# A decoder layer on one Trainium2 core: four-chunk groups with a PSUM bank a chunk, and the squares of x inside the opening group

## The chip, the cores and the metric

The kernel runs on one core of one Trainium2 chip. The metric is the time of one execution on the device, in microseconds (us); less is better. The engines are TensorE (PE in the profile; PEld is its weight load), VectorE (DVE), ScalarE (ACT), GpSimd (POOL) and SyncE (SP), whose queue issues most transfers.

## The reference

One layer of a decoder with 256 tokens of 1024 features, float32 throughout. Each of four sub-layers has an RMS norm before and after it, and is added to the residual stream:

```python
h = rmsnorm(x, ffn1_pre_g)                      # x * rsqrt(mean(x*x) + eps) * g
f = (silu(h @ w_gate) * (h @ w_up)) @ w_down    # D_FF = 2816
x = x + 0.5 * rmsnorm(f, ffn1_post_g)

h = rmsnorm(x, mix_pre_g)
proj = h @ w_in                                 # q, k, v (8 heads of 64) and pooling input
y = concatenate([moba_attention(q, k, v), multiscale_pool(p_in)]) @ w_out
x = x + rmsnorm(y, mix_post_g)

h = rmsnorm(x, xa_pre_g)                        # 4 heads of 256 over 256 memory tokens
x = x + rmsnorm(memory_cross_attention(h, rmsnorm(mem, mem_g)), xa_post_g)

# a second half-FFN like the first
```

## The kernel before, in words

Activations are held with features on partitions: a tensor of 1024 x 256 is eight chunks (ND = 8) of 128 features by 256 tokens (S). Every float32 operand of a product is split into a high and a low half, both in a reduced format (`fp32r`); a chunk of activations lies as 512 columns, high half in the first 256, low half in the other 256. A product of weight tile and chunk is then low weight x high activation, high weight x high activation and high weight x low activation.

**Weights** come as one stream of 128 x 128 tiles in the order in which they are used, in units of eight tiles (`UNIT`). The class `Weights` loads them (`_load`, on SP's queue), and `_make` (L76, L77) makes the high half by a cast on ScalarE and the low half by a subtraction on VectorE, some four units (`LEAD`) ahead of use. The first four units are loaded and split in parts by `open_in_parts` (L109, L112), together with the chunks of x (L188, L191).

**How products are formed.** `wide_chunk` makes one chunk of 128 output features in one PSUM bank: for two k at a time, two products of 256 columns by the low weights into the bank's second half (L210), then two of 512 columns by the high weights into the whole bank (L212). The second half is then added to the first, with a copy on ScalarE and an add on VectorE (L219, L220). `group` makes four chunks at a time, so that one k of the activations serves four tiles: two banks hold the four chunks, a half bank each, and a step of one k is twelve products of 256 columns (L266, L271, L273). There are three such groups, at the start of a stage, where the chunks of activations come one by one: the first two gate/up pairs of the first FFN (with the high weights first, since these are ready first), q of `w_in`, and four chunks of `xa_wq`. `row_step` forms products with the activations as weights and rows of 512 outputs, over four banks (L337 to L339).

**Norms.** The pre-norm's factor of a token isn't put into the activations; the products are scaled by it afterwards (`rBx`, made by `x_spread`). For the first FFN it comes from `x_squares` (three Squares on ScalarE, L579, and three adds on VectorE, L584) and `x_sums` (four products with a column of ones on TensorE, L590, and a root). `x_squares` is run in the code between the gate and the up half of f = 2, `x_sums` between those of f = 3, and `opened`, with `x_spread`, between those of f = 4.

**Order.** TensorE goes through its products in the order of the code everywhere. Between `seam(True)` and `seam(False)` all engines do; the opening, with its group, and the ends of rows (`row_end`, with the group that follows) lie there. Elsewhere a planner orders the other engines, by its own estimate of times. PSUM has eight banks: six in the pool of `accum`, two in that of `small`.

**Ends of rows.** `row_end` forms the post-norm of a stage, adds it to the residual, and transposes the result into the next stage's chunks: the first 128 tokens through small banks, the second 128 by `turned(i)`, four chunks at a time, between the halves of a filler pair of the memory tokens' keys.

`start` begins with seven plain products of zeros (`warm`, L542), each two passes in the trace, before the first weights are there.

Of the kernel before, what the change touches and what calls it, by code (L numbers as in the profile page):

```python
# [8 lines left out]
F32 = mybir.dt.float32  # L9
# [6 lines left out]
P = 128  # L16
D = 1024
S = 256
# [125 lines left out]
def build(nc, io, tiles_only=False):  # L144
# [3 lines left out]
    def small(name="sm"):  # L148
        return st["psm"].tile([P, 512], F32, name=name, tag="sm")

    def accum():
        return st["pacc"].tile([P, 512], F32, name="acc")

    def tmp(shape, name, **kw):
        return st["tmp"].tile(shape, F32, name=name, **kw)
# [28 lines left out]
    def halves(ps):  # L184
        return [ps[:, :S], ps[:, S:]]
# [21 lines left out]
    def wide(ps, ws, Xs, first, last):  # L207

        for i, (hi, lo) in enumerate(ws):
            nc.tensor.matmul(ps[:, S:], lo, Xs[i][:, :S], start=first and i == 0, stop=False, skip_group_check=True)  # L210
        for i, (hi, lo) in enumerate(ws):
            nc.tensor.matmul(ps, hi, Xs[i], start=False, stop=last and i == 1, skip_group_check=True)  # L212

    def wide_chunk(X, ps, o):

        for k in range(0, ND, 2):
            wide(ps, [st["w"].get() for _ in range(2)], [st[X][:, k + i, :] for i in range(2)], k == 0, k == ND - 2)
        c = tmp([P, S], "cmb")
        nc.scalar.copy(c, ps[:, S:])  # L219
        nc.vector.tensor_tensor(o, ps[:, :S], c, op=ALU.add)  # L220
# [37 lines left out]
    def group(name, X, cols, done, before=None, hi_first=False):  # L258

        def run():  # L260
            ps = [accum() for _ in range(2)]
            o = [h for p in ps for h in halves(p)]

            def by_lo(ws, k, first):
                for i, (hi, lo) in enumerate(ws):
                    nc.tensor.matmul(o[i], lo, st[X][:, k, :S], start=first and i % 2 == 0,  # L266
                                     stop=k == ND - 1 and hi_first, skip_group_check=True)

            def by_hi(ws, k, first):
                for i, (hi, lo) in enumerate(ws):  # L270
                    nc.tensor.matmul(o[i], hi, st[X][:, k, :S], start=first and i % 2 == 0,  # L271
                                     stop=False, skip_group_check=True)
                    nc.tensor.matmul(o[i], hi, st[X][:, k, S:], start=False,  # L273
                                     stop=k == ND - 1 and not hi_first, skip_group_check=True)
            steps = (by_hi, by_lo) if hi_first else (by_lo, by_hi)
            for k in range(ND):
                if before:
                    before(k)
                ws = [st["w"].get() for _ in cols]
                for i, by in enumerate(steps):  # L280
                    by(ws, k, k == i == 0)
            done(ps)
        names = [name] * len(cols) if isinstance(name, str) else name
        pr.add(run, [(n, k * P, c) for k in range(ND) for n, c in zip(names, cols)])
# [126 lines left out]
    def row_end(parts, ks, weights, factor, nxt, pre, fillers):  # L411
# [55 lines left out]
        def turned(i):  # L467
            def run():
                cs = range(4 * i, 4 * i + 4)
                x_turn(1, cs, accum)  # L470
                for c in cs:
                    x_hi(1, c)
                for c in cs:
                    x_lo(1, c)
            return run
# [54 lines left out]
    def start():  # L530
        X = st["xs_ffn1"] = xsplit()
        st["xf"] = keep([P, ND, S], "y")
        first = st["x0"] = st["ffn"].tile([P, 2 * S], F32, name="gu", bufs=6)
        n = S + len(GAINS) * ND
        nc.sync.dma_start(first[:, :n], io["first"])
        nc.gpsimd.memset(st["eps"], EPS)
        nc.gpsimd.memset(st["one"], 1.0)
        warm = tmp([P, S], "cmb")
        nc.vector.memset(warm, 0.0)
        ps = small("warm")  # L540
        for _ in range(7):
            nc.tensor.matmul(ps[:, :P], warm[:, :P], warm[:, :P], start=True, stop=True)  # L542

        def load(c):
            if c == 1:
                nc.scalar.preload_act_table(AF.Sqrt)
                nc.scalar.dma_start(st["xf"][:, 1:3, :], io["x"][:, 1:3, :])
            s = {2: slice(3, 5), 4: slice(5, 8)}.get(c)
            if s:
                nc.sync.dma_start(st["xf"][:, s, :], io["x"][:, s, :])  # L550

        def split(c):
            if c == 0:
                x, g = first[:, :S], first[:, S:S + 1]
                return (lambda: nc.vector.tensor_scalar(X[:, 0, :S], x, g, None, op0=ALU.mult),
                        lambda: (split_lo(X, 0, x, g), nc.vector.tensor_copy(st["gain"], first[:, S:n])))
            g = gain("ffn1_pre_g", c)
            return lambda: split_hi(X, c, st["xf"][:, c, :], g), lambda: split_lo(X, c, st["xf"][:, c, :], g)

        st["w"].open_in_parts(ND // 2, load, split)  # L560
        nc.scalar.dma_start(st["const"][:, :P], io["const"][:, :P])
        for g, w in enumerate(WINDOWS):
            nc.vector.tensor_scalar(st["half"][:, g:g + 1], gain("pool_scale", g), 1.0 / w, None, op0=ALU.mult)
# [12 lines left out]

    def x_squares():
        for o, x in ((st["xf"][:, 0, :], st["x0"][:, :S]), 2 * (st["xf"][:, 1:4, :],), 2 * (st["xf"][:, 4:8, :],)):
            st["tc"].keep_in_program_order(nc.scalar.activation(o, x, AF.Square))  # L579
        n = ND  # L580
        while n > 1:
            n //= 2
            x = st["xf"][:, :n, :]
            nc.vector.tensor_tensor(x, x, st["xf"][:, n:2 * n, :], op=ALU.add)  # L584

    def x_sums():

        ps = small("sums")
        for t in range(2):
            nc.tensor.matmul(ps[:, t:t + 1], st["xf"][:, 0, t * P:(t + 1) * P], st["one"], start=True, stop=True)  # L590
        inverse_root(ps[:, :2], "x")
# [39 lines left out]
    def ffn(n, X, before, aside, last):  # L631
# [16 lines left out]

        def finish(f, t):

            src = t
            if f < 2:
                t = st["ffn"].tile([P, 2, S], F32, name="gu", bufs=6)
                src = src.rearrange("p (i s) -> p i s", i=2)
            nc.vector.tensor_tensor(t, src, st["rBx"][:, None, :].to_broadcast([P, 2, S]), op=ALU.mult)  # L655

            def rest():
                nc.scalar.activation(t[:, 0, :], t[:, 0, :], AF.Silu)
                nc.vector.tensor_tensor(t[:, 0, :], t[:, 0, :], t[:, 1, :], op=ALU.mult)
                h = st["h", f] = st["ffn"].tile([P, 1, 2 * S], F32R, name="h", bufs=LAG + 4)  # L660
                split_plain(h, 0, t[:, 0, :])
            defer(rest)
# [51 lines left out]
            pr.add(lambda: row_step(st["h", k], 0, k == 0), [(wd, k * P, c * P) for c in range(ND)])  # L714

        if n == 1:
            group([wg, wu] * 2, X, [0, 0, P, P], early.extend, before=before, hi_first=True)
        else:
            row_group(*before)
        seam(False)  # L720
# [2 lines left out]
        for f in range(2, NF):  # L723
            gate, up = gate_up(f, early.append if f < first + 1 else lambda t, f=f: finish(f, t))
            pr.add(*gate)
            if f == 2 and n == 1:
                side(x_squares)
            if f == first and n == 1:
                side(x_sums)
            if f == first + 1:  # L730
                side(opened)
            if f == 5 and n == 2:
                side(turn_h)
            pr.add(*up)
            for run in aside.get(f, ()):
                pr.add(run)
            held = {2: [], 3: [], 4: [], 5: [0], 6: [1, 2], 7: [3]} if n == 1 else {2: [], 3: [], 4: [], 5: [], 6: [0, 1], 7: [2, 3]}
            for k in held.get(f, [f - LAG]):
                down(k)
# [284 lines left out]
    side(post_load, 1)  # L1024
    held = {}

    group("w_in", "xs_mix", [c * P for c in range(4)], lambda ps: held.update(q=ps), before=run)
    seam(False)
    wide_pair("w_in", "xs_mix", [4 * P, 5 * P], lambda ps: held.update(k=ps), lambda: side(x_root))
    table(AF.Exp)  # L1030
    side(x_spread)

    def q_out():
        for i, ps in enumerate(held["q"]):
            scaled_pair("qk", 2 * i, ps)
        scaled_pair("qk", 4, held["k"])

    def enter_mix():
# [58 lines left out]
            st[n] = st["xa"].tile([P, 2, D], F32R, name=n)  # L1097
    pr.add(enter_xa)
    side(post_load, 2)
    group("xa_wq", "xs_xa", [c * P for c in range(4)], lambda ps: held.update(q=ps), before=run)  # L1100
    seam(False)

    def xq_out():
        st["xs_q"] = xsplit()
        for i, ps in enumerate(held["q"]):
            split_pair(st["xs_q"], 2 * i, ps)

    def xq_root():
        x_root()
        rq = st["rq"] = keep([P, 2], "rq")  # L1110
        nc.vector.tensor_scalar(rq, st["rx"], 1.0 / 16, None, op0=ALU.mult)
    side(xq_out)
    side(xq_root)
    table(AF.Exp)
    for c in (4, 6):
# [143 lines left out]
```

## Time and profile before

| | us |
|---|---|
| three timed runs: median (lowest to highest) | 571.16 (569.06 to 573.45) |
| the profiled execution's own time | 568.8 |
| its span, first to last instruction | 567.0 |
| TensorE busy in it | 558.4 |
| VectorE busy | 410.0 |
| ScalarE busy | 347.6 |

The profile is of one execution. Busy times of engines overlap each other; a product's printed duration also overlaps the next one's, so what a product costs is read from the spacing of starts.

### The profile page before, as it was taken

The numbers are of one execution on the slowest core, as the hardware profiler recorded it, in microseconds if no ns is written. First come the engines' busy times: TensorE is split into PE (matmuls) and PEld (weight loads), VectorE is DVE, ScalarE is ACT, GpSimd is POOL, SyncE is SP. The second block draws the span as 40 slices with busy tenths as digits, with TensorE's granted clock in tenths as the row PEclk, the third lists the DMA queues.
The fourth block names the chain that finished last, engine by engine and source line by source line (L and its number), as shares of the span: only waits on it lengthen the run. The fifth ranks groups of instructions, "written<-read, shape, count | busy, mean of one in ns | idle before, by whom it ended". The sixth has DMA issues, their size and how long they took to land.

```text
span 567.0 us, 8164 instructions
## 1 busy us (share of the span) xinstructions
PE 558.4 (98%) x3130; PEld 484.1 (85%) x3130; DVE 410.0 (72%) x679; ACT 347.6 (61%) x632; POOL 19.7 (3%) x34
## 2 busy tenths in 40 slices
PE   9899999999999999999999999999999999999996
PEld 8788888888888898888899888888888888888884
DVE  6798777778776797985498676367986776776644
ACT  6688675555557685775388566358754555555542
POOL 0000000000000000580000000000000000000000
PEclk9999999999999999999999999999999999999999
DMA  8995856545554196084068444422965556454102
GB/s 317 353 371 190 321 218 238 223 159 214 169 202 149 40 342 227 24 296 149 1 235 323 149 148 149 138 86 89 351 221 194 188 183 222 156 216 163 62 0 74
DMA packets 29110, 107.00 MB, mean 189 GB/s; under 512 B 1936, under 2 KB 2832, under 8 KB 28688
## 3 DMA queue, kind: packets, MB, share of 16 engines
q1 hardware_dynamic: 28496, 105.97, 52.2%
q10 hardware_dynamic: 576, 0.52, 0.3%
q8 instruction: 24, 0.39, 0.3%
q14 instruction: 14, 0.11, 0.1%
HBM read 105.44 MB, written 1.05 MB: 188 GB/s over the span
## 4 chain that ended last, share of the span: by engine, by line
PE 94%; DMA 2%; DVE 1%; ACT 1%; issue 1%; SPq 0%; DVEq 0%
PE acc L212 18%; PE sm L212 13%; PE acc L337 10%; PE acc L339 10%; PE acc L338 10%; PE acc L210 9%; PE sm L210 6%; DMA wraw<-w 2%; PE acc L301 2%; PE acc L299 2%; PE acc L300 2%; PE acc L273 1%; PE acc L271 1%; PE acc L266 1%; PE acc L180 1%; PE acc L182 1%
## 5 line engine op out<-in xcount | busy, mean ns | idle before, releaser
L77 DVE TENSOR_TENSOR wlo<-wraw,whi 128x1024 fp32r<-128x1024 f32 x184 | 223.4, 1222 | 68.9 <-ACT whi L76 68.4
L76 ACT CAST whi<-wraw 128x1024 fp32r<-128x1024 f32 x184 | 192.5, 1054 | 42.9 <-PE acc L339 35.2
L212 PE MATMUL acc<-xs,whi 128*128 128x512 f32 x448 | 140.7, 395 | 0.0
L212 PE MATMUL sm<-xs,whi 128*128 128x512 f32 x320 | 100.5, 395 | 0.0
L210 PEld LDWEIGHTS acc<-xs,wlo 128*128 128x128 f32 x448 | 83.6, 188 | 19.2
L210 PE MATMUL acc<-xs,wlo 128*128 128x256 f32 x448 | 88.4, 279 | 0.0
L210 PEld LDWEIGHTS sm<-xs,wlo 128*128 128x128 f32 x320 | 59.8, 188 | 13.9
L337 PE MATMUL acc<-whi,h 128*128 128x512 f32 x176 | 68.6, 390 | 0.0
L339 PE MATMUL acc<-whi,h 128*128 128x512 f32 x176 | 68.5, 389 | 0.0
L338 PE MATMUL acc<-wlo,h 128*128 128x512 f32 x176 | 68.5, 389 | 0.0
L212 PEld LDWEIGHTS acc<-xs,whi 128*128 128x128 f32 x448 | 68.2, 189 | 0.0
L210 PE MATMUL sm<-xs,wlo 128*128 128x256 f32 x320 | 63.2, 279 | 0.0
L219 ACT COPY cmb<-acc 128x256 f32<-128x256 f32 x56 | 20.8, 371 | 62.1 <-PE acc L212 62.0
L212 PEld LDWEIGHTS sm<-xs,whi 128*128 128x128 f32 x320 | 48.7, 189 | 0.0
L219 ACT COPY cmb<-sm 128x256 f32<-128x256 f32 x40 | 14.9, 373 | 48.8 <-PE sm L212 48.7
L338 PEld LDWEIGHTS acc<-wlo,h 128*128 128x128 f32 x176 | 33.0, 188 | 7.0
L337 PEld LDWEIGHTS acc<-whi,h 128*128 128x128 f32 x176 | 33.0, 188 | 7.0
L339 PEld LDWEIGHTS acc<-whi,h 128*128 128x128 f32 x176 | 33.0, 188 | 7.0 <-DVE h L196 0.2
L220 DVE TENSOR_TENSOR gu<-acc,cmb 128x256 f32<-128x256 f32 x40 | 16.9, 423 | 18.2 <-ACT cmb L219 18.1
L220 DVE TENSOR_TENSOR gu<-sm,cmb 128x256 f32<-128x256 f32 x40 | 17.0, 424 | 16.9 <-ACT cmb L219 16.9
L655 DVE TENSOR_TENSOR gu<-gu,rBx 128x512 f32<-128x512 f32 x40 | 27.6, 691 | 1.1
L337 PE MATMUL acc<-whi,xs 128*128 128x512 f32 x64 | 25.3, 395 | 0.0
(206 smaller groups left out, 788.9 us busy)
## 6 DMA issues: line engine op xcount, KB each, us to landing
wraw<-w SPq DMA_DIRECT2D x91, 1024.0 KB, 4.8
post<-post SPq DMA_DIRECT2D x4, 512.0 KB, 5.3
wraw<-w SPq DMA_DIRECT2D x7, 256.0 KB, 5.0
wraw<-w SPq DMA_DIRECT2D x2, 512.0 KB, 6.3
y<-memt SPq DMA_DIRECT2D x1, 1024.0 KB, 4.8
y<-mem SPq DMA_DIRECT2D x1, 1024.0 KB, 6.8
xt<-xt SPq DMA_DIRECT2D x1, 1024.0 KB, 8.3
out_dram<-y SPq DMA_DIRECT2D x3, 256.0 KB, 2.0
```

The lines of the kernel that those rows point to most:

```text
L76: self.nc.scalar.copy(hi, raw)
L77: eng.tensor_tensor(lo, raw, hi.bitcast(F32), op=ALU.subtract)
L210: nc.tensor.matmul(ps[:, S:], lo, Xs[i][:, :S], start=first and i == 0, stop=False, skip_group_check=True)
L212: nc.tensor.matmul(ps, hi, Xs[i], start=False, stop=last and i == 1, skip_group_check=True)
L219: nc.scalar.copy(c, ps[:, S:])
L220: nc.vector.tensor_tensor(o, ps[:, :S], c, op=ALU.add)
L299: nc.tensor.matmul(box[t], a, hi, start=k == 0, stop=False)
L300: nc.tensor.matmul(box[t], a, lo, start=False, stop=False)
L337: nc.tensor.matmul(o, a, hi, start=first, stop=False, skip_group_check=True)
L338: nc.tensor.matmul(o, a, lo, start=False, stop=False, skip_group_check=True)
L339: nc.tensor.matmul(o, b, hi, start=False, stop=last, skip_group_check=True)
L655: nc.vector.tensor_tensor(t, src, st["rBx"][:, None, :].to_broadcast([P, 2, S]), op=ALU.mult)
```

## The change

- `group` takes a bank for each chunk (four instead of two). A step of one k is then, for each chunk, one product of 256 columns by the low weight into the second half of the bank and one of 512 by the high weight into the whole bank, as in `wide_chunk`. In the opening group's first step the 512 columns stay two products of 256, and that step is done for chunks 0 and 1 and then for 2 and 3, each with high weights before low ones.
- The two halves of each bank are added up right behind the group (`add_up`, split off from `wide_chunk`), inside the region of fixed order: into the tiles of gate and up (opening group), into `qk` (`q_sums`), and into a buffer of two chunks that is split at once (`xq_sums`). `finish` and `q_out` then work in place on these.
- `x_squares` is run at k = 4 of the opening group, before that step's weights are fetched. `x_sums` takes a bank of `accum`.
- `turned(1)` takes a bank of `small` instead of `accum`.
- Eight warming products instead of seven.

```diff
--- before.py
+++ after.py
@@ -215,6 +215,9 @@
 
         for k in range(0, ND, 2):
             wide(ps, [st["w"].get() for _ in range(2)], [st[X][:, k + i, :] for i in range(2)], k == 0, k == ND - 2)
+        add_up(ps, o)
+
+    def add_up(ps, o):
         c = tmp([P, S], "cmb")
         nc.scalar.copy(c, ps[:, S:])
         nc.vector.tensor_tensor(o, ps[:, :S], c, op=ALU.add)
@@ -258,27 +261,28 @@
     def group(name, X, cols, done, before=None, hi_first=False):
 
         def run():
-            ps = [accum() for _ in range(2)]
-            o = [h for p in ps for h in halves(p)]
-
-            def by_lo(ws, k, first):
-                for i, (hi, lo) in enumerate(ws):
-                    nc.tensor.matmul(o[i], lo, st[X][:, k, :S], start=first and i % 2 == 0,
+            ps = [accum() for _ in cols]
+
+            def by_lo(both, k, first):
+                for o, (hi, lo) in both:
+                    nc.tensor.matmul(o[:, S:], lo, st[X][:, k, :S], start=first,
                                      stop=k == ND - 1 and hi_first, skip_group_check=True)
 
-            def by_hi(ws, k, first):
-                for i, (hi, lo) in enumerate(ws):
-                    nc.tensor.matmul(o[i], hi, st[X][:, k, :S], start=first and i % 2 == 0,
-                                     stop=False, skip_group_check=True)
-                    nc.tensor.matmul(o[i], hi, st[X][:, k, S:], start=False,
+            def by_hi(both, k, first):
+                order = [(c, slice(0, 2 * S)) for c in both]
+                if first:
+                    order = [(c, p) for p in (slice(0, S), slice(S, 2 * S)) for c in both]
+                for (o, (hi, lo)), p in order:
+                    nc.tensor.matmul(o[:, p], hi, st[X][:, k, p], start=first and p.start == 0,
                                      stop=k == ND - 1 and not hi_first, skip_group_check=True)
             steps = (by_hi, by_lo) if hi_first else (by_lo, by_hi)
             for k in range(ND):
                 if before:
                     before(k)
-                ws = [st["w"].get() for _ in cols]
-                for i, by in enumerate(steps):
-                    by(ws, k, k == i == 0)
+                both = [(o, st["w"].get()) for o in ps]
+                for part in ([both[:2], both[2:]] if hi_first and k == 0 else [both]):
+                    for i, by in enumerate(steps):
+                        by(part, k, k == i == 0)
             done(ps)
         names = [name] * len(cols) if isinstance(name, str) else name
         pr.add(run, [(n, k * P, c) for k in range(ND) for n, c in zip(names, cols)])
@@ -467,7 +471,7 @@
         def turned(i):
             def run():
                 cs = range(4 * i, 4 * i + 4)
-                x_turn(1, cs, accum)
+                x_turn(1, cs, (accum, small)[i])
                 for c in cs:
                     x_hi(1, c)
                 for c in cs:
@@ -538,7 +542,7 @@
         warm = tmp([P, S], "cmb")
         nc.vector.memset(warm, 0.0)
         ps = small("warm")
-        for _ in range(7):
+        for _ in range(8):
             nc.tensor.matmul(ps[:, :P], warm[:, :P], warm[:, :P], start=True, stop=True)
 
         def load(c):
@@ -576,7 +580,7 @@
 
     def x_squares():
         for o, x in ((st["xf"][:, 0, :], st["x0"][:, :S]), 2 * (st["xf"][:, 1:4, :],), 2 * (st["xf"][:, 4:8, :],)):
-            st["tc"].keep_in_program_order(nc.scalar.activation(o, x, AF.Square))
+            nc.scalar.activation(o, x, AF.Square)
         n = ND
         while n > 1:
             n //= 2
@@ -585,7 +589,7 @@
 
     def x_sums():
 
-        ps = small("sums")
+        ps = accum()
         for t in range(2):
             nc.tensor.matmul(ps[:, t:t + 1], st["xf"][:, 0, t * P:(t + 1) * P], st["one"], start=True, stop=True)
         inverse_root(ps[:, :2], "x")
@@ -648,11 +652,7 @@
 
         def finish(f, t):
 
-            src = t
-            if f < 2:
-                t = st["ffn"].tile([P, 2, S], F32, name="gu", bufs=6)
-                src = src.rearrange("p (i s) -> p i s", i=2)
-            nc.vector.tensor_tensor(t, src, st["rBx"][:, None, :].to_broadcast([P, 2, S]), op=ALU.mult)
+            nc.vector.tensor_tensor(t, t, st["rBx"][:, None, :].to_broadcast([P, 2, S]), op=ALU.mult)
 
             def rest():
                 nc.scalar.activation(t[:, 0, :], t[:, 0, :], AF.Silu)
@@ -714,7 +714,13 @@
             pr.add(lambda: row_step(st["h", k], 0, k == 0), [(wd, k * P, c * P) for c in range(ND)])
 
         if n == 1:
-            group([wg, wu] * 2, X, [0, 0, P, P], early.extend, before=before, hi_first=True)
+            def opened_group(ps):
+                for i in (0, 2):
+                    t = st["ffn"].tile([P, 2, S], F32, name="gu", bufs=6)
+                    for j in range(2):
+                        add_up(ps[i + j], t[:, j, :])
+                    early.append(t)
+            group([wg, wu] * 2, X, [0, 0, P, P], opened_group, before=lambda k: k == 4 and x_squares(), hi_first=True)
         else:
             row_group(*before)
         seam(False)
@@ -723,8 +729,6 @@
         for f in range(2, NF):
             gate, up = gate_up(f, early.append if f < first + 1 else lambda t, f=f: finish(f, t))
             pr.add(*gate)
-            if f == 2 and n == 1:
-                side(x_squares)
             if f == first and n == 1:
                 side(x_sums)
             if f == first + 1:
@@ -1024,15 +1028,18 @@
     side(post_load, 1)
     held = {}
 
-    group("w_in", "xs_mix", [c * P for c in range(4)], lambda ps: held.update(q=ps), before=run)
+    def q_sums(ps):
+        for i, p in enumerate(ps):
+            add_up(p, st["qk"][:, i, :])
+    group("w_in", "xs_mix", [c * P for c in range(4)], q_sums, before=run)
     seam(False)
     wide_pair("w_in", "xs_mix", [4 * P, 5 * P], lambda ps: held.update(k=ps), lambda: side(x_root))
     table(AF.Exp)
     side(x_spread)
 
     def q_out():
-        for i, ps in enumerate(held["q"]):
-            scaled_pair("qk", 2 * i, ps)
+        for i in (0, 2):
+            scaled_pair("qk", i, st["qk"][:, i:i + 2, :].rearrange("p i s -> p (i s)"))
         scaled_pair("qk", 4, held["k"])
 
     def enter_mix():
@@ -1097,19 +1104,20 @@
             st[n] = st["xa"].tile([P, 2, D], F32R, name=n)
     pr.add(enter_xa)
     side(post_load, 2)
-    group("xa_wq", "xs_xa", [c * P for c in range(4)], lambda ps: held.update(q=ps), before=run)
+    def xq_sums(ps):
+        st["xs_q"] = xsplit()
+        for i in (0, 2):
+            t = tmp([P, 2 * S], "wide", bufs=1)
+            for j in range(2):
+                add_up(ps[i + j], t[:, j * S:(j + 1) * S])
+            split_pair(st["xs_q"], i, t)
+    group("xa_wq", "xs_xa", [c * P for c in range(4)], xq_sums, before=run)
     seam(False)
-
-    def xq_out():
-        st["xs_q"] = xsplit()
-        for i, ps in enumerate(held["q"]):
-            split_pair(st["xs_q"], 2 * i, ps)
 
     def xq_root():
         x_root()
         rq = st["rq"] = keep([P, 2], "rq")
         nc.vector.tensor_scalar(rq, st["rx"], 1.0 / 16, None, op0=ALU.mult)
-    side(xq_out)
     side(xq_root)
     table(AF.Exp)
     for c in (4, 6):
```

## Rows read from the trace of the kernel before

**Rows 1.** The page: TensorE's busy time, granted clock by slice, and the chain by engine

```profile
PE 558.4 (98%) x3130; PEld 484.1 (85%) x3130; DVE 410.0 (72%) x679; ACT 347.6 (61%) x632; POOL 19.7 (3%) x34
...
PEclk9999999999999999999999999999999999999999
...
PE 94%; DMA 2%; DVE 1%; ACT 1%; issue 1%; SPq 0%; DVEq 0%
```

**Rows 2.** Waits of TensorE: who waited for whom, total us, times, longest

```profile
PE sums L590 <- DVE y L584: 2.0, 1, 2.0
PE acc L773 <- ACT diag L772: 1.8, 1, 1.8
```

**Rows 3.** The chain that ended last, 9 to 31 us: start, duration, what

```profile
10.01 8.31 DMA wraw<-w
```

**Rows 4.** Timeline to 40 us, start, duration, engine; then L579, L584 (min/median/max ns)

```profile
13.16 2.20 ACT L76 CAST whi<-wraw 128x1024 fp32r<-128x1024 f32 x2
...
18.34 2.00 ACT L76 CAST whi<-wraw 128x1024 fp32r<-128x1024 f32 x2 [2.98 <-DMA wraw<-w]
...
19.42 2.36 DVE L77 TENSOR_TENSOR wlo<-wraw,whi 128x1024 fp32r<-128x1024 f32 x2 [2.70 <-ACT whi L76]
...
22.40 0.42 PEld L210 LDWEIGHTS acc<-xs,wlo 128*128 128x128 f32 x2
...
L579 ACT ACTIVATE y<-y x2: 837/947/1057, 20.8 to 22.5; 128x768 f32<-128x768 f32 x1, 128x1024 f32<-128x1024 f32 x1
...
L584 DVE TENSOR_TENSOR y<-y x3: 417/686/1219, 23.8 to 27.0; 128x1024 f32<-128x1024 f32 x1, 128x512 f32<-128x512 f32 x1, 128x256 f32<-128x256 f32 x1
```

**Rows 5.** Timeline of TensorE, 25 to 28.4 us

```profile
24.95 0.63 PE L212 MATMUL acc<-xs,whi 128*128 128x512 f32 x2
27.54 0.58 PE L590 MATMUL sums<-one,y 128*128 128x1 f32 x4 [1.96 <-DVE y L584]
```

**Rows 6.** Timeline of TensorE, 192 to 222 us: a group's step, then wide steps

```profile
200.94 0.64 PE L266 MATMUL acc<-xs,wlo 128*128 128x256 f32 x4
...
202.38 0.64 PE L266 MATMUL acc<-xs,wlo 128*128 128x256 f32 x4
...
211.02 0.40 PE L210 MATMUL acc<-xs,wlo 128*128 128x256 f32 x2
...
216.61 0.61 PE L325 MATMUL pb<-const,rcx 128*128 128x128 f32 x4
```

**Rows 7.** Timeline of TensorE, 62 to 64.3 us: row products of 512 columns

```profile
62.21 0.39 PE L339 MATMUL acc<-whi,h 128*128 128x512 f32 x1
62.44 0.39 PE L337 MATMUL acc<-whi,h 128*128 128x512 f32 x1
...
62.89 0.39 PE L339 MATMUL acc<-whi,h 128*128 128x512 f32 x1
```

**Rows 8.** Timeline, 0 to 9 us: the warming products, the first products and casts

```profile
1.18 3.06 PEld L542 LDWEIGHTS warm<-cmb 128*128 128x128 f32 x14 [1.18 <-DVE cmb L539]
...
4.58 0.28 PEld L271 LDWEIGHTS acc<-xs,whi 128*128 128x128 f32 x1 [0.34 <-ACT whi L109]
...
5.26 0.41 PE L271 MATMUL acc<-xs,whi 128*128 128x256 f32 x1
...
5.48 0.35 PE L273 MATMUL acc<-xs,whi 128*128 128x256 f32 x1
...
6.20 0.62 ACT L109 CAST whi<-wraw 128x512 fp32r<-128x512 f32 x1
...
6.87 0.19 PEld L271 LDWEIGHTS acc<-xs,whi 128*128 128x128 f32 x1
...
7.64 0.62 ACT L109 CAST whi<-wraw 128x512 fp32r<-128x512 f32 x1 [0.41 <-DMA wraw<-w]
```

**Rows 9.** Timeline of ScalarE and VectorE, 211 to 219 us: an add-up behind the group

```profile
214.02 0.37 ACT L219 COPY cmb<-acc 128x256 f32<-128x256 f32 x1 [1.74 <-PE acc L212]
...
214.42 0.43 DVE L220 TENSOR_TENSOR wide<-acc,cmb 128x256 f32<-128x256 f32 x1 [0.88 <-ACT cmb L219]
```

## The prediction

> **What bounds the kernel now.** The page first: TensorE is busy 98% of the span and 94% of the chain that ended last are its products [rows 1]. So only two things can shorten this kernel: fewer or shorter products, or less waiting on TensorE. Next, its list of waits: at L590, the sums of the squares of x, it stood still for 2.0 us, and the only other wait past the first products is 1.8 us in the last rows [rows 2], which the change does not touch. The chain of waits then says why L590 was late: it runs back through a load of weights in flight from 10.01 us for 8.31 us [rows 3]. The reader should see in the timeline how that load comes to stand before a sum of x: the Squares were put on ScalarE behind the cast that waited 2.98 us for this load, and the adds on VectorE lie between the halves of weights that follow it [rows 4]. Last, TensorE's own rows, for the spacing of starts, which is what a product costs here; the printed durations overlap [rows 6, 7].
>
> **Part 1: the Squares go into the opening group.** They are written at k = 4, where all engines keep program order: on ScalarE after the casts of units 4 and 5, which end at 15.36, before that of unit 6, which waits for its load until 18.34 [rows 4]. Their inputs are long there, because all splits of x are written before the group. The two large Squares take 0.84 and 1.06 us [rows 4], the first, of 256 columns, some 0.4 as a copy of that size does [rows 9], so 2.3 us: 15.4 to about 17.7, inside a gap of 2.98. The cover is that gap; without it the casts of unit 6 and later ones would come 2.3 us later. The three adds (1.22, 0.69, 0.42 [rows 4]) follow on VectorE, some 17.7 to 20.0, in front of the low half of unit 6, which stood at 19.42 and now starts at about 20 and ends at 21.2. That unit's first weights went into the array at 22.40 [rows 4], by 0.25 earlier now (part 2): about 1 us of spare. The sums are then ready 5 us before TensorE comes to them. How much does the wait give back? The two wide products before it start at 24.95 and take 0.227 each (part 2), so L590 could start at 25.40; it started at 27.54 [rows 5]. That the step from wide products to plain ones costs nothing more is seen at 216.61, which is within 0.05 of where eight wide steps should end [rows 6]. So 2.1 us come back; the list's own figure for the wait, 2.0, counts from the modelled end and is the lower bound [rows 2]. I take **2.1**. What is late next? Behind the sums TensorE goes to the up half of f = 3, whose unit 7 is made right behind unit 6 (ready near 22.4, used near 25.6). The sums now free x's buffer earlier too, so the load of the memory tokens, which SP held for it, is issued some 2 us earlier, as everything behind it is: no cost. The sums take a large bank instead of a small one; four of the six large ones are being emptied then, see part 3.
>
> **Part 2: a bank a chunk.** Before, a step of a group is 12 products of 256 columns in 1.44 us (200.94 to 202.38), so 0.120 each [rows 6]. Now the two by the high half become one of 512. A wide step of the existing kind, two of 256 and two of 512, comes eight times between 211.02 and 216.61, so it takes 0.699 us where six of 256 would take 0.72 [rows 6]. It holds two merged pairs: 0.0106 us for each. The other reading, 512 columns alone, starts every 0.2267 us (62.21 to 62.89 is three) [rows 7], against 2 x 0.120: 0.0133 us a pair. The groups hold 3 x 8 x 4 = 96 pairs of (step, chunk); the four of the opening group's first step stay split, so 92 are merged: 1.0 to 1.2 us, and I take 1.1.
>
> The opening group can't keep all of its third. Its second step starts at 6.87, 0.05 after the cast that it needs ends (6.20 + 0.62), and the third, 1.44 later at 8.31, against 7.64 + 0.62 = 8.26 [rows 8]: until there it goes at the pace of ScalarE. So one step of the seven gives nothing: -0.04. A merged product also needs both halves of its chunk of x at its start, not 0.12 later; those stood in time, so nothing to -0.1. With that, **1.0** for all three groups.
>
> A rule of the Trainium skill differs here: TensorE: Matmul & The Clock Gate, section "Wait — 56ns, not 53.3ns?", puts the fixed cost of a product at some 2.5 ns, so the 92 pairs would give an estimated 0.23 us. The rows say 11 to 13 ns a pair.
>
> **Part 3: what the banks cost.** The groups add four add-ups each: a copy on ScalarE of 0.37 and an add on VectorE of 0.43 [rows 9], so 1.5 and 1.7 us. In the opening group they replace nothing that TensorE waits for; they stand behind the low half of unit 7 (near 22.4) and end near 24. TensorE needs one of these banks first for the sums, at 25.2, or, if the allocator prefers a bank in use to the sixth, for f = 3 at 22.2: 0 to -0.5, and I take nothing. In w_in's group ScalarE sat idle 1.74 us right behind the group [rows 9], room for the copies. In xa_wq's there is a chain, since the buffer of two chunks is single: a copy and two adds, a split of 512 columns on both engines, then the same for the other pair. With a split at twice a copy and twice an add, that is 2 x (0.37 + 2 x 0.43 + 0.74 + 0.86) = 5.7 us, an estimate, in which the cast of a unit four ahead may stand behind it. Four units are four chunks of 2.8 us [rows 6]: 11 us of cover, so nothing, and at worst 0.5. The turned half in a small bank leaves six large ones: four for the group, one for the filler's pair, one for the first turned half; nothing, as long as the first half of the rows is split by then, and I have no row that speaks against it.
>
> **Part 4: a warming product more.** Two more passes at 0.22 (3.06 us for 14) push the end of the warm weight loads from 4.24 to about 4.7; the first product's load stood at 4.58 after 0.34 idle [rows 8]. The first step now runs lo products of chunks 0 and 1 in the gap before the second piece of weights, worth up to 0.24, and loses 0.1 at its start. Both fall into the wait for the cast that ends at 6.82. Bounds -0.2 to +0.2; I take 0.
>
> **The sum.** 2.1 + 1.0 = 3.1 us. The profiled execution took 568.8 us, with a span of 567.0 and 1.8 around it: 565.7, with a span of 563.9. The three timed runs have their median at 571.16, 2.4 above the profiled one, and I put the same gain there: 568.1 us, 0.5% less. One per cent of this kernel is 5.7 us, about the least that a measurement of it tells from no change; the gain is below that.
>
> **Rivals.** (a) *The merged products give nothing*, because the weight load of each chunk, not the columns, sets the pace, or because four banks come late at a seam and eat it: only 2.1 stays, 569.1. For it: 256 columns cost 0.120, over half of 0.2267. Against: the wide steps show the merged pace already [rows 6]. (b) *The wait is not gone but moved*: the adds are fixed on VectorE in front of the low halves of units 6 and 7, and TensorE waits for those. The spare is about 1 us. If the Squares start 2.3 us later than I think, unit 6 is whole near 23.5 and TensorE, which wants it near 22.15, stands for 1.35: 3.1 - 1.35 = 1.75 stays, 569.4. If they stand behind the cast of unit 6 after all, it is whole near 25.3 and the new wait of 3.1 eats the gain: 571.2. For it: these adds now come ahead of weights that are due, where before they came between weights that had time. Against: the gap of 2.98 lies where the code puts the Squares [rows 4]. (c) *Slower: changing the bank with every product.* A step now changes bank eight times, not four: 96 changes more. At s each, the gain is gone from s = 3.1 / 96 = 32 ns, and beyond that the kernel is slower. Against: the product at 62.44 goes to another bank than the one at 62.21 and comes 0.23 behind it, where the mean is 0.227 [rows 7], which leaves room for a few ns. Worse would be pauses that lower the granted clock: if the groups ran at the spacing of 0.22 that the first products show (5.26 to 5.48) [rows 8] instead of 0.120, their 24 steps of 1.44 would take 29 us more, 597. The Trainium skill has such a case (TensorE: Matmul & The Clock Gate, "A second HAM failure mode: psum-queue depth-cycling": products that cycle through banks paused often enough for the clock to drop and rise). No row here shows one: the granted clock is 9 or more tenths in all 40 slices, with row products over four banks in most of them [rows 1].
>
> **Chances and range.** The forecast 0.68; (a) 0.12; (b) 0.12; (c) 0.03; something that gives more than 1%, such as waits that the engines' new order takes away elsewhere, 0.05. The forecast's bounds, 2.4 to 3.4 us, are narrower than the spread of the three runs (569.06 to 573.45): the low end of the range is the lowest run less 3.4, 565.7, a little lower for the last case, 565.3; the high end is (b) with the gain eaten, 571.2, which is also the highest run less 2.3. Faster by over 1%: 0.07; within 1%: 0.89; slower: 0.04.
>
> **What would show it.** The wait at L590 gone, the Squares on ScalarE at 15 to 18 us and no wait in their place at the up half of f = 3; the group steps at 1.39 to 1.40 us instead of 1.44, the opening group's third step still at 8.3; the first products of the pairs behind the groups without idle time; the span near 563.9. It is wrong if TensorE has a new wait above 0.5 us in 16 to 45 us or at the seams, if the groups' steps stay at 1.44 or grow, or if the granted clock leaves its upper level in a group.

## The result, and the profile after

| | before | after |
|---|---|---|
| timed runs, median (lowest to highest) | 571.85 (569.06 to 573.45), 6 runs | 566.17 (565.89 to 566.34), 6 runs |
| the profiled execution | 568.8 | 565.89 |
| its span | 567.0 | 564.1 |

The ratio of the runs is 0.9922, with a 95% interval of 0.9899 to 0.9944: 0.8% less time (the two medians of the table alone lie 1.0% apart; over more runs the median of before is lower, see below). The forecast was 568.1 us and a gain of 3.1 us. The profile shows 2.9 us; the timed runs show more, and the times of after lie within 0.5 us of one another where those of before are spread over 4.4. That difference is what the experiments are for.

The page of the changed kernel: TensorE, granted clock by slice, and the chain by engine.

```profile
PE 557.2 (99%) x3040; PEld 479.3 (85%) x3040; DVE 413.7 (73%) x691; ACT 349.8 (62%) x643; POOL 19.8 (4%) x34
...
PEclk9999999999999999999999999999999999999998
...
PE 98%; DMA 1%; DVE 0%; ACT 0%; SPq 0%; issue 0%; DVEq 0%
```

TensorE has 90 products fewer than in [rows 1] (92 pairs are merged, and the eighth warming product adds two passes), and holds 98% of the chain instead of 94%: the load of 8.31 us [rows 3] and the adds of the squares are off it. Its waits in the changed kernel (who waited for whom, total, times, longest):

```profile
PE acc L777 <- ACT diag L776: 1.8, 1, 1.8
PE warm L546 <- DVE cmb L543: 1.2, 1, 1.2
PE acc L276 <- ACT whi L109: 0.2, 1, 0.2
```

The row of the sums in [rows 2] has no successor. The timeline of the changed kernel, up to 45 us and around the group of `w_in`: start, duration, engine.

```profile
6.85 1.19 PE L276 MATMUL acc<-xs,whi 128*128 128x512 f32 x4
...
9.75 1.09 PE L276 MATMUL acc<-xs,whi 128*128 128x512 f32 x4
...
11.23 1.20 PE L276 MATMUL acc<-xs,whi 128*128 128x512 f32 x4
...
16.92 0.40 PE L210 MATMUL acc<-xs,wlo 128*128 128x256 f32 x2
...
24.83 0.63 PE L212 MATMUL acc<-xs,whi 128*128 128x512 f32 x2
25.29 0.50 PE L594 MATMUL acc<-one,y 128*128 128x1 f32 x4
...
10.56 0.62 ACT L109 CAST whi<-wraw 128x512 fp32r<-128x512 f32 x1 [1.18 <-DMA wraw<-w]
...
13.86 2.20 ACT L76 CAST whi<-wraw 128x1024 fp32r<-128x1024 f32 x2
...
16.27 1.78 ACT L583 ACTIVATE y<-y 128x768 f32<-128x768 f32 x2
17.96 1.99 ACT L76 CAST whi<-wraw 128x1024 fp32r<-128x1024 f32 x2
...
18.09 2.41 DVE L588 TENSOR_TENSOR y<-y 128x1024 f32<-128x1024 f32 x3 [0.67 <-ACT y L583]
20.41 2.36 DVE L77 TENSOR_TENSOR wlo<-wraw,whi 128x1024 fp32r<-128x1024 f32 x2
...
197.08 0.72 PE L268 MATMUL acc<-xs,wlo 128*128 128x256 f32 x4
197.64 1.09 PE L276 MATMUL acc<-xs,whi 128*128 128x512 f32 x4
198.57 0.64 PE L268 MATMUL acc<-xs,wlo 128*128 128x256 f32 x4
...
199.97 0.64 PE L268 MATMUL acc<-xs,wlo 128*128 128x256 f32 x4
...
208.37 0.40 PE L210 MATMUL acc<-xs,wlo 128*128 128x256 f32 x2
```

The Squares end at 18.05 and the adds at 20.5, so the sums, at 25.29 against 27.54 [rows 5], find their input ready and come 2.25 us earlier. Not all of that is the wait: the last wide products ahead of the sums start at 24.83 against 24.95 [rows 5], so 0.12 was there before. From these products to the sums it took 2.59 us and takes 0.46, so the wait gave back 2.13.

In the group of `w_in` a step takes 1.40 us (198.57 to 199.97) against 1.44 [rows 6]; the wide steps behind it come 2.65 us earlier (208.37 against 211.02), and 0.3 more, the gain of `xa_wq`'s group, makes up the 2.9 of the span. The opening group kept the 0.12 of its third and no more: its second step starts where it did (6.85 against 6.87 [rows 8]), at 11.23 it waited for a cast that had waited 1.18 us for its weights, and the wide steps behind it start at 16.92. In the kernel before they start here:

```profile
17.04 0.40 PE L210 MATMUL acc<-xs,wlo 128*128 128x256 f32 x2
```

### The profile page after: what moved, and what is told of

It reads as the page before. It is cut to its first block, busy times and chain, and to the rows that moved or that the text cites. A ratio compares the mean times of both kernels' runs of the same rounds, so it can differ in the third digit from the quotient of the medians.

```text
span 564.1 us, 8020 instructions
## 1 busy us (share of the span) xinstructions
PE 557.2 (99%) x3040; PEld 479.3 (85%) x3040; DVE 413.7 (73%) x691; ACT 349.8 (62%) x643; POOL 19.8 (4%) x34
## 4 chain that ended last, share of the span: by engine, by line
PE 98%; DMA 1%; DVE 0%; ACT 0%; SPq 0%; issue 0%; DVEq 0%
PE acc L212 18%; PE sm L212 13%; PE acc L341 10%; PE acc L343 10%; PE acc L342 10%; PE acc L210 9%; PE sm L210 7%; PE acc L276 4%; PE acc L305 2%; PE acc L303 2%; PE acc L304 2%; PE acc L268 2%; DMA wraw<-w 1%; PE sm L400 1%; PE acc L180 1%; PE acc L182 1%
## 5 line engine op out<-in xcount | busy, mean ns | idle before, releaser
L222 ACT COPY cmb<-acc 128x256 f32<-128x256 f32 x68 | 24.7, 372 | 57.1 <-PE acc L212 56.5
L223 DVE TENSOR_TENSOR gu<-acc,cmb 128x256 f32<-128x256 f32 x44 | 18.4, 423 | 19.0 <-ACT cmb L222 19.0
L655 DVE TENSOR_TENSOR gu<-gu,rBx 128x512 f32<-128x512 f32 x42 | 28.8, 690 | 1.1
L276 PE MATMUL acc<-xs,whi 128*128 128x512 f32 (+1 forms) x100 | 26.6, 388 | 0.3 <-ACT whi L109 0.2
```

Source lines behind the costliest of these rows:

```text
L276: nc.tensor.matmul(o[:, p], hi, st[X][:, k, p], start=first and p.start == 0, stop=k == ND - 1 and not hi_first, skip_group_check=True)
L655: nc.vector.tensor_tensor(t, t, st["rBx"][:, None, :].to_broadcast([P, 2, S]), op=ALU.mult)
```

## The experiments

A line number moves by a few from kernel to kernel; the sums are L590 to L596. Ratios are to the kernel before, run beside each, with their 95% intervals. The changed kernel was not run beside the edits to it, so a difference to its 566.17 is one between series; two edits of it that change nothing that can be told gave 565.94 and 566.03, so some 0.2 us of such a difference says nothing. Spans of single traces differ for another reason too: the wide steps behind the opening group start between 16.73 and 17.68 us, and in the three latest of these traces (17.55 and more) TensorE had waited for a cast of the first weights.

**The kernel before, once more**, without an edit.

> The kernel before, unchanged, against itself: it shows how far two series of the same kernel lie apart, and gives a second profile. Theory A (the wait of TensorE for the sums of squares is as long as the load of unit 6 is late, and that differs from execution to execution): ratio 1.000 within 0.003, single times spread over 3 to 4 us, and the wait at L590 is another than 2.0 us, with the span longer or shorter by the same amount. Theory B (the spread of the times of before has nothing to do with this wait): the wait is again 2.0 us within 0.2, whatever the span is.

Ratio 0.9986 (0.9967 to 1.0005); median 569.45 of 12 runs, beside 570.54 of 23. The profiled execution was one of the shortest (span 567.0), so it could not tell the theories apart. In its list of waits:

```profile
PE sums L590 <- DVE y L584: 1.8, 1, 1.8
```

So one profile says little on the spread. But each run is listed with its mean granted clock (1 is the upper level), and over the 72 runs of before that were taken for these experiments the times go with it:

```
mean granted clock   runs   lowest   median   highest (us)
0.998 and more         25   568.49   569.00   569.88
0.997                  13   568.69   569.12   572.16
0.994 to 0.996         29   569.99   570.64   572.29
0.993 and less          5   572.43   572.97   573.31
```

Not every long run has a low clock: four runs at 0.997 took 570.8 to 572.2 us.

**The Squares alone.** Before, with the Squares in the opening group; groups, banks and warming products as they were.

```diff
-            st["tc"].keep_in_program_order(nc.scalar.activation(o, x, AF.Square))
+            nc.scalar.activation(o, x, AF.Square)
...
-            if f == 2 and n == 1:
-                side(x_squares)
...
-            group([wg, wu] * 2, X, [0, 0, P, P], early.extend, before=before, hi_first=True)
+            group([wg, wu] * 2, X, [0, 0, P, P], early.extend, before=lambda k: k == 4 and x_squares(), hi_first=True)
```

> Before, with only the Squares and adds moved to k = 4 of the opening group. Theory A: the wait at L590 is gone, the span is 565.0 within 0.4 (567.0 less 2.0), and the times lie close together (within 1 us), so that the ratio to before is 0.9925 to 0.995, more than the 2.0 us of the first profile, 0.9965, would give. Theory B: ratio 0.9965, and a spread of 3 us or more stays. Theory C (the larger gain of the timed runs comes from the banks or from the eighth warming product): ratio 0.9965 with a small spread of neither origin.

Ratio 0.9938 (0.9916 to 0.996), median 567.28 (566.91 to 567.76); span 566.0. The spread is gone with the wait, as theory A has it; the span fell by 1.0 only, where 2.0 was expected. The timeline of TensorE shows why. The opening group ended late in this trace: the wide steps behind it start at 17.65 us, where they start at 17.04 before and at 17.10 in the next run, which has the same Squares. And behind the sums TensorE waits again:

```profile
17.65 0.40 PE L210 MATMUL acc<-xs,wlo 128*128 128x256 f32 x2
...
26.02 0.50 PE L590 MATMUL sums<-one,y 128*128 128x1 f32 x4
26.92 0.50 PE L210 MATMUL sm<-xs,wlo 128*128 128x256 f32 x2 [0.40 <-DVE gu L220]
```

The product behind the sums wants a small bank. There are two, the sums hold one, and the other still holds the up half of f = 2.

**Squares, and the sums in a large bank.** The kernel above with

```diff
-        ps = small("sums")
+        ps = accum()
```

> Before, with the Squares at k = 4 and the sums in a large bank; groups, turned half and seven warming products as before. In the run with the sums in a small bank, the up half of f = 3 waited 0.4 us (some 0.7 us in starts) for the small bank of the up half of f = 2. Theory A: that wait goes, and the time is 0.6 to 0.8 us below that run's median of 567.28, 566.6 within 0.2. Rival: the up half then waits for its weights or the next bank, and the time stays at 567.2 within 0.2.

566.76 (566.47 to 567.21), ratio 0.994 (0.9917 to 0.9963), span 564.8, and no such wait: from the sums to the next product it takes 0.37 us in the trace, where it took 0.90 (26.02 to 26.92). The bank of the sums was worth 0.5 us, in the traces and in the medians of the two series.

**The banks alone.** The changed kernel with the Squares back between the halves of f = 2.

```diff
-            nc.scalar.activation(o, x, AF.Square)
+            st["tc"].keep_in_program_order(nc.scalar.activation(o, x, AF.Square))
...
-            group([wg, wu] * 2, X, [0, 0, P, P], opened_group, before=lambda k: k == 4 and x_squares(), hi_first=True)
+            group([wg, wu] * 2, X, [0, 0, P, P], opened_group, hi_first=True)
...
+            if f == 2 and n == 1:
+                side(x_squares)
```

> The changed kernel with the Squares where they were (between the halves of f = 2), so banks, small bank and eighth warming product alone. Theory A: the wait at L590 is back (1.5 us or more), the spread of 3 us or more is back, and the ratio to before is 0.998 within 0.002 (0.6 to 1.0 us of shorter products). Theory C: most of the gain stays, ratio 0.994 or less, with a small spread.

Slower: 573.65 (571.93 to 575.21), ratio 1.0056 (1.0037 to 1.0075). Neither theory had that. The wait and the spread are back, as theory A has it, and all 12 runs have a mean clock of 0.996 or less. Its timeline around the sums, and then the busy time of TensorE in four stretches (start and end, length, PE busy, granted clock, DMA share, GB/s):

```profile
17.80 2.01 ACT L76 CAST whi<-wraw 128x1024 fp32r<-128x1024 f32 x2 [1.69 <-DMA wraw<-w]
...
24.14 1.79 ACT L583 ACTIVATE y<-y 128x768 f32<-128x768 f32 x2
...
29.73 0.58 PE L594 MATMUL acc<-one,y 128*128 128x1 f32 x4 [3.52 <-DVE y L588]
...
30.95 0.48 PE L210 MATMUL sm<-xs,wlo 128*128 128x256 f32 x2
...
32.08 0.63 PE L210 MATMUL sm<-xs,wlo 128*128 128x256 f32 x2
...
33.36 0.63 PE L210 MATMUL sm<-xs,wlo 128*128 128x256 f32 x2
...
34.60 0.40 PE L210 MATMUL acc<-xs,wlo 128*128 128x256 f32 x2
```

```profile
26.20:29.70 3.50, 0.01 (x1) 1.00 1.03 406
29.70:30.95 1.25, 1.22 (x8) 1.00 0.47 193
30.95:34.60 3.65, 3.65 (x13) 0.53 0.80 294
34.60:38.00 3.40, 3.40 (x23) 1.00 1.01 416
```

Two things are to be seen. The group's add-ups, now fixed in the opening, and the casts between them push the two large Squares further back (from 24.14; in [rows 4] from 20.8), so the wait is 3.5 us. The load of unit 6 is not the cause here: its cast starts at 17.80, earlier than in [rows 4] (18.34). And some time behind it the granted clock is 0.53, next to the lower level (1.2 of 2.4 GHz): three wide steps take 3.65 us where three of 0.70 would take 2.1, so another 1.5 us are lost behind the wait. That suggested the next experiment.

**Products in the wait.** Before, and the kernel of the banks alone, with eight products that fill a part of the wait:

```diff
+        for _ in range(8):
+            nc.tensor.matmul(ps[:, :P], st["ident"], st["ident"], start=True, stop=True)
```

> Before, with eight products of the unit matrix by itself ahead of the sums (their results are overwritten), so that TensorE works for some 1.4 us of the time in which it stood still. Theory A1 (the executions of before that take 570 to 573 us are those in which the granted clock falls behind the wait at L590): the Squares are as late as before, the fastest executions stay at 568.5 to 569, but the slow ones go: median 568.9 within 0.4, spread below 2 us, no mean clock below 0.997, ratio 0.997 within 0.002. Theory A2 (only the length of the wait differs, by when the load lands): nothing changes, median 570.5, spread 4 us. Theory D (the clock falls for a reason elsewhere in the kernel): mean clocks of 0.991 to 0.996 stay.

> The changed kernel with the Squares where they were, as in the run of the banks alone, and the eight products of the unit matrix ahead of the sums. There, the wait at L594 was 3.5 us and the products behind it ran at a granted clock of 0.54 for 3.7 us. Theory A1: the clock stays at its upper level behind the wait, worth 0.46 of 3.7 us, so the median falls from 573.65 by 1.2 to 2 us, to about 572, and no mean clock is below 0.996. Theory A2 or D: median 573.65 within 0.5, clocks of 0.991 to 0.994.

In before: 569.16 (568.62 to 570.72), and no mean clock below 0.997 in 12 runs, where 7 of the 19 beside it were at 0.996 or less and reached 573.02. The spread of 2.1 us is a little more than theory A1 allows, and two runs at a clock of 0.998 still took 570.4 and 570.7. The median is 0.6 lower, the ratio, 0.9989 (0.9972 to 1.0006), not clear of 1. In the other kernel the expectation failed: 573.6, with clocks of 0.991 to 0.996. Its stretches say why: the eight products end at 27.05, 2.39 us of standing still are left, and behind them the clock was at the lower level for 6.56 us. In before with the same products 0.3 us were left, and the clock stayed up.

```profile
27.93 0.58 PE L592 MATMUL sums<-one,y 128*128 128x1 f32 x4 [0.34 <-DVE y L584]
...
28.00:33.00 5.00, 5.00 (x31) 1.00 0.65 235
```

The two stretches of the other kernel:

```profile
27.05:29.44 2.39, 0.00 (x1) 0.97 0.94 329
29.44:36.00 6.56, 6.56 (x23) 0.50 0.76 286
```

**A late load.** Both kernels with 512 KB that nobody needs ahead of the load of unit 6:

```diff
         self._load(n_units + 1, 1)
+        self.extra()
...
+            st["w"].extra = lambda: nc.sync.dma_start(st["xt"][:, 0, :], io["xt"][:, 0, :])
```

> Before, with 512 KB of the residual rows loaded early on SP's queue, ahead of the load of unit 6 (they are loaded again later, so the output is the same). At some 400 GB/s that makes the load of unit 6 and all behind it some 1.3 us later. Theory A (the wait for the sums is as long as that load is late): the wait at L590 is 3.0 to 3.6 us instead of 1.8 to 2.0, and with it the clock falls behind it in most executions: median 571.5 to 573.5. Rival (the wait is set by the amount of work on ScalarE and VectorE, not by the load): wait 2.0 within 0.3, median within 0.5 of before.

> The changed kernel with the same early load. Theory A (the Squares stand ahead of the cast that waits for the load, so nothing on the way to the sums waits for it): no wait at the sums, times within 1 us of one another, at most 0.5 us above the changed kernel's 566.17; only a wait for unit 6 itself at the gate of f = 3 could come, since its spare was about 1 us. Rival: slower by the 1.3 us or more.

Before becomes slower, 571.76 (570.22 to 573.1), ratio 1.0033 (1.0018 to 1.0048), with 9 of 12 runs at a clock of 0.996 or less. Its cast of unit 6 waits longer for the load than the 2.98 of [rows 4], its sums come later than the 27.54 of [rows 5], and the clock falls behind them:

```profile
19.54 2.01 ACT L76 CAST whi<-wraw 128x1024 fp32r<-128x1024 f32 x2 [3.75 <-DMA wraw<-w]
...
28.74 0.58 PE L591 MATMUL sums<-one,y 128*128 128x1 f32 x4 [3.00 <-DVE y L585]
```

```profile
30.20:33.54 3.34, 3.34 (x13) 0.51 0.89 316
```

The changed kernel isn't touched: 566.03 (565.85 to 566.28). Its cast of unit 6 is as late, and its sums wait for nothing:

```profile
19.16 2.00 ACT L76 CAST whi<-wraw 128x1024 fp32r<-128x1024 f32 x2 [0.85 <-DMA wraw<-w]
...
25.54 0.50 PE L595 MATMUL acc<-one,y 128*128 128x1 f32 x4
```

**Not merged.** The changed kernel with the split form of the first step in all steps (`if first:` becomes `if True:` in `by_hi`).

> The changed kernel with every group's products by the high weights kept as two of 256 columns, over four banks: first all four chunks with the high half of x, then all four with the low half, so every product changes the bank. Theory A (the merge is worth 0.011 to 0.013 us a pair, a change of bank nothing): the steps take 1.44 us, 0.6 to 1.2 us more than the changed kernel, 566.8 to 567.4. Rival (c) of the prediction (a change of bank costs): the steps take more than 1.46 us, at 32 ns a change over 2 us more than that. If the merge gave nothing: 566.2, steps of 1.40.

566.82 (566.45 to 567.18), 0.65 us above the changed kernel; a step takes 1.44 us, with another bank for every product:

```profile
10.03 1.12 PE L276 MATMUL acc<-xs,whi 128*128 128x256 f32 x8
10.99 0.64 PE L268 MATMUL acc<-xs,wlo 128*128 128x256 f32 x4
11.47 1.12 PE L276 MATMUL acc<-xs,whi 128*128 128x256 f32 x8
```

**Seven warming products** instead of eight, in the changed kernel (`range(7)`).

> The changed kernel with seven warming products. Theory A: the same as the changed kernel within 0.2 us, about 564.1 of span and 566.2 of time: the first step waits for casts in both. Theory C, as far as it is the warming product: slower than the changed kernel by 1 us or more, or times that spread over more than 1 us.

565.94 (565.86 to 566.22): no difference that can be told.

**Both turned halves in large banks**, in the changed kernel (`x_turn(1, cs, accum)`).

> The changed kernel with both turned halves in large banks again. Theory A (the small bank is needed so that four large ones are free when the two later groups start): the group's fourth chunk waits for the bank of the first turned half, which VectorE has read at 197.66, against a start of that chunk near 197.4, so 0.3 to 0.6 us at each of two seams, 566.8 to 567.4. Rival (the bank is free in time, the edit is worth nothing): 566.2 within 0.2.

567.01 (566.66 to 567.41), 0.84 us above the changed kernel. The first step of `w_in`'s group lasts 0.94 us up to its wide products, against 0.56 above (197.08 to 197.64), and `xa_wq`'s group has the same. Its list of waits has a row that the changed kernel has not, the weights of these steps behind the read of the turned half (L425):

```profile
197.74 1.10 PE L268 MATMUL acc<-xs,wlo 128*128 128x256 f32 x4
198.68 1.09 PE L276 MATMUL acc<-xs,whi 128*128 128x512 f32 x4
...
PEld acc L268 <- DVE xs L425: 0.6, 2, 0.3
```

## Why the prediction was right, and where it was not

**Part 1, the wait**, was right in its mechanism and, for the profile, in its size. The Squares went into the gap, the wait is gone, nothing took its place: 2.13 us for 2.1 forecast. But "I put the same gain there", for the timed runs, failed. Of the 1.9 us by which 568.1 was too long, 1.1 is the base, the median of three runs (571.16, where 72 runs have 570.1), and 0.8 is the gain. The wait is not the same in every kernel and execution: with the order of work as it was it grows with the lateness of the load of unit 6 (the late load made it 3.0 us and left the changed kernel alone), and the order of work alone made it 3.5. In the three traces in which TensorE stood still longer than in the profiles of before, the granted clock fell behind it. Of the 72 runs of before, 34 had a mean clock of 0.996 or less; their medians, 570.64 and 572.97, are 1.6 and 4.0 above the 569.0 of the 25 with the highest clock. Against those 25 the changed kernel gains 2.8 us, about what the profile shows; against all 72, whose median is 570.1, 3.9 us. The prediction read "the granted clock is 9 or more tenths in all 40 slices" from an execution in which it had not fallen, and took the spread of the three timed runs for noise. That the clock makes the difference between the shorter and the longer runs is likely and not shown: no trace of the kernel before itself has the clock low. It rests on the correlation, on three traces of edited kernels, and on the products in the wait, which ended the low clocks in before but moved its median by less than its interval; how much of a longer run is the wait and how much the clock was not separated run by run.

**Part 1, the large bank for the sums**, on which part 3 says "0 to -0.5, and I take nothing": it costs nothing, and is a needed piece worth 0.5 us (567.28 to 566.76). The prediction looked at who needs the large banks, and not at who gets a small one back.

**Part 2, the merge**: 0.65 us in the medians for 1.0. The step of 1.40 us is as forecast, and the two later groups give 2 x 8 x 0.04 = 0.64, or 10 ns for each of their 64 pairs, where the forecast took 12 (some 0.77 us). Of the opening group's third the forecast kept some 0.2; the profile shows 0.12, and its pace is that of the casts and of their loads: from its second step to the wide steps it takes 10.07 us in the trace of the changed kernel (6.85 to 16.92) and 9.9 to 10.6 in those of the edits that have merged steps, against 10.17 before (6.87 to 17.04). The fixed cost of 2.5 ns a product of the Trainium skill (TensorE: Matmul & The Clock Gate, section "Wait — 56ns, not 53.3ns?") would have made it an estimated 0.16 for those two groups' 64 pairs; the steps show four times that, and the measurement decides.

**Part 3, the banks of the seams**: no wait came, as forecast. That the small bank for the turned half is what prevents it (0.84 us) was seen as a condition only, without a price.

**Part 4, the warming product**: 0, as forecast.

**The rivals.** (a) fell: the merge gives. (b) fell: unit 6's low half began at 20.41, and the spare of the forecast was enough even when its load came late. (c) fell: twelve changes of bank in a step of the kernel that isn't merged take the 1.44 us that four took before, so a change costs nothing that can be seen, and the changed kernel's clock stays up in all slices of its groups. The case that the Trainium skill tells of in TensorE: Matmul & The Clock Gate, "A second HAM failure mode: psum-queue depth-cycling", is not met here. The stretch of `w_in`'s group, at a clock of 1.00:

```profile
197.08:208.37 11.29, 11.29 (x68) 1.00 0.95 340
```

Where the clock did fall, it was in kernels with the late Squares, and behind one wait. A mechanism that the prediction lacked is that the parts depend on one another: the banks without the early Squares are 0.6% slower than before.

## What to carry to other kernels

A spread of times that one kernel has and its neighbour has not is evidence: list the runs by their granted clock before calling it noise, since the one profile may be of the best case. Work that TensorE waits for late belongs ahead of anything that waits for a load, on every engine that it passes; moving it there was worth the wait and its variation here, and probably the clock behind it. When a bank is taken or given back, follow who gets the next one of that pool, and price the edit by undoing it.

## What the runs showed of the hardware

After TensorE had stood still for 2.4 us (the banks with products in the wait), 3.0 us (the late load) and 3.5 us (the banks alone), the granted clock was at 0.50 to 0.53 for 6.6, 3.3 and 3.7 us, one trace each: the shortest standstill has the longest stretch, so its length alone does not tell what follows; after the 2.0 and 1.8 us in the two profiles of before it stayed at its upper level. In the second and third case 1.2 to 1.5 us of products still ran at the upper level first.
